# Feature transposes in the attention's banks, and an earlier scale for w_gu, in a one-core hybrid attention and mLSTM step

## The chip, the cores and the metric

The kernel runs on one core of a Trainium2 chip. The metric is the device time of one execution in microseconds (us), lower is better; the kernel before takes 1528.98 us as the median of three runs (1525.18 to 1530.79).

The core has five engines with an instruction queue each, executed in order: TensorE (PE in the profile, with its weight loads listed apart as PEld), VectorE (DVE), ScalarE (ACT), GpSimd (POOL) and SyncE (SP), which in this kernel mostly issues transfers. Results of matmuls land in PSUM, eight banks of 512 float32 values per partition, and are read from there by DVE or ACT. A bank that holds something unread can't take the next product.

## The reference

One layer of a diffusion backbone on 128 context tokens and 1024 latent tokens, width 1024, all in float32:

```
h   = rmsnorm(x) * (1 + sc1) + sh1
aq, ak, av, mq, mk, mv, mo, mg = split(h @ w_in)
o   = softmax(rope(aq) . rope(keys)) . vals          # 8 query heads, 2 key/value heads of 64
hm  = mlstm(mq, mk, mv, mg), both directions         # 4 heads of 128, chunks of 128 tokens
x   = x + g1 * (concat(o, rmsnorm(hm) * sigmoid(mo)) @ w_out)
h2  = rmsnorm(x) * (1 + sc2) + sh2
g, u = split(h2 @ w_gu)                              # 2 x 2816 columns
x   = x + g2 * ((silu(g) * u) @ w_down)
y   = rmsnorm(x)
```

Returned are y for both groups of tokens and, for the context, the keys and values and the mLSTM states. Float32 accuracy is kept by splitting an operand into a high part and a low rest and adding three products (high times high, high times low, low times high).

## The kernel before

The 1152 tokens are nine blocks of 128, in three chunks of three blocks. Chunk 0 holds the context block; in the code the chunks' rows are `cur` (chunk 0), `nxt` (chunk 1) and `far` (chunk 2).

**The order of the instructions.** The kernel is a Python program that emits instructions; a planner then fixes the order on every engine when the program is built. It simulates the engines with its own costs and takes, where several instructions are ready, the one that was emitted first. `with hot(n)` makes instructions count as if emitted n instructions earlier. PSUM banks and SBUF buffers are slots of pools; a tile waits for its slot until all readers of the tile before it are through. At run time the order is fixed and every engine waits at the head of its queue. Which pieces of work are emitted next to each other is written by hand: `weave(main, side, n_main, n_side)` goes through the steps of `main`, each of which reports its size in units, and after each draws as many steps from `side` as are due, n_side for n_main units.

**The feed-forward of chunk 0** (`groups`) goes in five groups of 4, 4, 4, 5 and 5 column blocks f. For each f, `gate_up` makes two products (L1473 to L1475, 24 matmuls of 384 tokens each, 6 units), each in a bank of its own, then tanh on ACT (L1491), two DVE steps (L1492, L1493) that read both banks, and the split of the result (L1496 and L145). After each group `down` (L1215 to L1217) multiplies with w_down in two halves of 512 columns; a half of five column blocks is 45 matmuls in three blocks of 15: block 0 first, then blocks 1 and 2 side by side in two banks. In steps it reports, the first three belong to block 0 and the last three to blocks 1 and 2. `add_gated` (L1204, L1205) reads the bank and adds to the rows.

**Weights** come in pieces: a transfer into one of two raw buffers, a rounding copy on ACT (L174), the rest on DVE (L145). Five pieces have a home at a time. For w_gu, ACT also sums absolute values of each piece (L178, `jk`, into `wsum`), with a line from the pool `t2`, which has three buffers and also holds the normalised half lines `y` of the features and the products of `add_gated`.

**The second feed-forward**, of chunks 1 and 2 together, works on both chunks with seven products of half-size operands in float16 (`pair6`, L1620 to L1622) instead of eight. It needs two things. `features6` turns each block's normalised rows over: for each half of 512 columns ACT scales a line y (L1554), four PE transposes (L124) put it into one PSUM bank, and ACT and DVE read four pieces of it into F (L1562, L1564); sums and differences of the chunks' F go to the operand tile Bt. `weights6` makes the weights' sums and, with a common scale, their float16 parts (L1606, L1607). That scale is made by `weight_scale`: a maximum over wsum (L1540), a PE transpose of it, a maximum over the result (L200), four tiny DVE steps (L190 to L193), a product that spreads the result over the partitions (L204), a copy (L205) and three more tiny steps (L1542 to L1544).

**PSUM.** During the attention and until the end of chunk 0's feed-forward the eight banks are: three for the scores S of one head (`psum["S"]`), one for the attention's product with the values (`psum["po"]`), and four that `bank()` hands out in turn to everything else. The attention of the last chunk of queries (`att`) is emitted in full before the part that the diff touches; its probabilities are turned by transfers (phT, plT), and its output is read from po by ACT (L1156) and DVE (L1158).

**The part that changes** is woven so: `main` is group 4 of chunk 0 (90 units), the gate/up of group 5 (60 units) and the first half of its down products (15 units), 165 in all. `side` is some empty steps (fillers), then `feats`: `features6` for the three blocks of nxt (12 steps), the output projection of far (`attn_out`, L1251 to L1255, 7 steps), and `features6` for the three blocks of far (18 steps). After it come the second half of the down products, the scale, the first weights of the second feed-forward and that feed-forward itself.

Of the kernel before, what the change touches and what calls it, by code (L numbers as in the profile page):

```python
# [8 lines left out]
F32 = mybir.dt.float32  # L9
# [10 lines left out]
P = 128  # L20
# [16 lines left out]
GROUPS = [(0, 4), (4, 4), (8, 4), (12, 5), (17, 5)]  # L37
# [5 lines left out]
NG = 3  # L43
# [6 lines left out]
def hybrid_step(ctx: ExitStack, tc: tile.TileContext, I: dict, O: dict):  # L50
# [11 lines left out]
    def nm(s):  # L62
        uid[0] += 1
        return f"{s}_{uid[0]}"

    def weave(main, side, n_main, n_side):

        due = 0.0
        for units in main:
            due += n_side / n_main * (units or 1)  # L70
            while due >= 1.0:
                next(side, None)
                due -= 1.0

    def emit(gen):
        for _ in gen:
            pass

    def chain(*gens):
        for g in gens:  # L80
            for v in g:
                yield v
# [22 lines left out]
    psum = {"mm": es_b.enter_context(tc.tile_pool(name="pB", bufs=4, space=PSUM, reuse_waits="tile"))}  # L105
# [3 lines left out]
    def bank():  # L109
        turn_of[0] += 1  # L110
        at = psum["mm"] if "mm1" not in psum or turn_of[0] % 4 else psum["mm1"]
        return at.tile([P, 512], F32, name=nm("mm"), tag="mm")
# [31 lines left out]
    def sub(out, full, hi, eng):  # L144
        (dve if eng == "dve" else pool).tensor_tensor(out=out, in0=full, in1=hi, op=ALU.subtract)  # L145
# [11 lines left out]
    def load_piece(srcs, shape, raw=None, own=None, tally=None):  # L157

        a, b = shape
        n = a * b  # L160

        def view(t):
            return t[:, :n].rearrange("p (a b) -> p a b", b=b)

        raw = raw_tile() if raw is None else raw
        if not own:
            loaded["n"] = (loaded["n"] + 1) % len(piece_tags)
            tag = piece_tags[loaded["n"]]
            at = homes.get(tag, wp)
            own = [at.tile([P, 1024], F32R, name=nm(t), tag=tag, bufs=2) for t in ("whi", "wlo")]  # L170
        hi, lo = own
        for part, ap_ in srcs:
            loaded["piece"] = dma(part(view(raw)), ap_).ins
        nc.scalar.copy(hi[:, :n], raw[:, :n])  # L174
        sub(lo[:, :n], raw[:, :n], hi[:, :n].bitcast(F32), "dve")
        if tally is not None:
            jk = ft.tile([P, D], BF16, name=nm("jk"), tag="t2", bufs=nt2[0])
            act(jk[:, :n], hi[:, :n].bitcast(F32), AF.Abs, accum_out=wsum[:, tally : tally + 1])  # L178
        return view(hi), view(lo)
# [160 lines left out]
    ps = bank()  # L340
# [3 lines left out]
    ps = bank()  # L344
# [1132 lines left out]
    def gate_up(a, f0, nf):  # L1477
        th, tl = a["h2"]
        acts = a["act"] = []
        for f in range(f0, f0 + nf):  # L1480
            if True:
                pg, pu = bank(), bank()
                for off, ps in ((0, pg), (D_FF, pu)):
                    src = w_gu[f + (NF if off else 0)].rearrange("p (k n) -> p k n", k=KD)
                    wh, wl = load_piece([(full_view, src)], (KD, P), tally=2 * f + (off > 0))
                    products(ps[:, 0:CT], wh, wl, th, tl)
                    yield 6
                parts = [(slice(0, CT), pg[:, 0:CT], pu[:, 0:CT])]
            tn = fp.tile([P, CT], F32, name=nm("tn"), tag="tn", bufs=2)
            for cs, g, u in parts:  # L1490
                act(tn[:, cs], g, AF.Tanh, scale=0.5)  # L1491
                dve.scalar_tensor_tensor(out=tn[:, cs], in0=tn[:, cs], scalar=1.0, in1=u, op0=ALU.add, op1=ALU.mult)  # L1492
                dve.tensor_tensor(out=tn[:, cs], in0=tn[:, cs], in1=g, op=ALU.mult)  # L1493
            hl = hlp.tile([P, 2, CT], F32R, name=nm("hl"), tag="hl", bufs=5)
            ah, al = hl[:, 0], hl[:, 1]
            nc.scalar.copy(ah, tn)  # L1496
            sub(al, tn, ah.bitcast(F32), "pool")
            acts.append((ah, al))

    def down(c, a, f0, nf, n):  # L1500
        g = gate_bc(1, c, n)
        acts = a["act"]
        pieces = []
        for j in range(0, nf, 2):
            m = min(2, nf - j)
            rows = w_down[(f0 + j) * P : (f0 + j + m) * P, n * 512 : (n + 1) * 512].rearrange("(a p) n -> p a n", p=P)
            pieces.append(load_piece([(full_view, rows)], (m, 512)))
        yield from three_blocks(
            lambda k, i: (acts[k][0][:, i * P : (i + 1) * P], acts[k][1][:, i * P : (i + 1) * P]),
            pieces, nf, lambda i, ps: add_gated(a["x1"][i], ps, g(c * CB + i), n))  # L1510
# [27 lines left out]
    def weight_scale():  # L1538

        dve.tensor_reduce(out=six[:, 7:8], in_=wsum, axis=AX.X, op=ALU.max)  # L1540
        emit(power_scale(fp, ones, six[:, 7:8], six[:, 2:4]))
        dve.tensor_tensor(out=six[:, 4:5], in0=six[:, 1:2], in1=six[:, 3:4], op=ALU.mult)  # L1542
        dve.tensor_tensor(out=six[:, 6:7], in0=six[:, 4:5], in1=six[:, 4:5], op=ALU.mult)
        dve.tensor_scalar(out=six[:, 5:6], in0=six[:, 4:5], scalar1=0.5, scalar2=None, op0=ALU.mult)  # L1544

    def features6(a, c, i, Bt, firsts):

        x1, r = a["x1"][i], a["rs"][i]
        at = slice(i * P, (i + 1) * P)
        F = a4p.tile([P, KD, P], F32, name=nm("F"), tag="A4", bufs=7)  # L1550
        for half in range(2):
            with hot(600):
                y = t2()
                act(y, x1[:, half * 512 : (half + 1) * 512], AF.Copy, scale=r)  # L1554
                ps = bank()
                for j in range(4):
                    transpose(ps[:, j * P : (j + 1) * P], y[:, j * P : (j + 1) * P])
                for j in range(4):
                    k = half * 4 + j
                    s, t = mods6[:, k, 0:1], mods6[:, k, 1:2]  # L1560
                    if j == 0:
                        act(F[:, k], ps[:, j * P : (j + 1) * P], AF.Identity, scale=s, bias=t)  # L1562
                    else:
                        dve.tensor_scalar(out=F[:, k], in0=ps[:, j * P : (j + 1) * P], scalar1=s, scalar2=t, op0=ALU.mult, op1=ALU.add)  # L1564
            yield
        for half, b in ((0, B11), (1, B21)) if c == 1 else ((1, B22),):
            v = F[:, half * 4 : half * 4 + 4]
            with hot(600):
                nc.scalar.copy(Bt[:, b, 0, :, at], v)
                sub(Bt[:, b, 1, :, at], v, Bt[:, b, 0, :, at], "dve")  # L1570
            yield
        if c == 1:
            firsts.append(F)
            return
        first = firsts.pop(0)
        T = sp.tile([P, 4, 4, P], F32, name=nm("T"), tag="S", bufs=1)
        with hot(600):
            dve.tensor_tensor(out=T[:, T1], in0=first[:, 0:4], in1=F[:, 0:4], op=ALU.subtract)
            dve.tensor_tensor(out=T[:, T2], in0=F[:, 4:8], in1=T[:, T1], op=ALU.add)
            dve.tensor_tensor(out=T[:, T3], in0=F[:, 0:4], in1=F[:, 4:8], op=ALU.subtract)  # L1580
            dve.tensor_tensor(out=T[:, T4], in0=first[:, 4:8], in1=T[:, T2], op=ALU.subtract)
        yield
        for j in (0, 2):
            with hot(600):
                nc.scalar.copy(Bt[:, j : j + 2, 0, :, at], T[:, j : j + 2])
                sub(Bt[:, j : j + 2, 1, :, at], T[:, j : j + 2], Bt[:, j : j + 2, 0, :, at], "dve")
            yield
# [162 lines left out]
    ps = bank()  # L1750
# [36 lines left out]
    cur, nxt = {}, {}  # L1787
# [11 lines left out]
    def groups(c, a, lst):  # L1799
        for f0, nf in lst:  # L1800
            yield from gate_up(a, f0, nf)
            yield from down(c, a, f0, nf, 0)
            yield from down(c, a, f0, nf, 1)
# [13 lines left out]
    main = groups(0, cur, GROUPS[:NG])  # L1817
    with tc.issue_after(loaded["gate"]):
        for _ in range(4):
# [10 lines left out]
    firsts = []  # L1830
    feats = chain(*[features6(nxt, 1, i, Bt, firsts) for i in range(CB)],
                  attn_out(far, o2, g_d[0, 1], lambda i: mixing(a4p, "A4", 7), o_d[CB:]), *[features6(far, 2, i, Bt, firsts) for i in range(CB)])
    main = chain(groups(0, cur, GROUPS[NG:-1]), gate_up(cur, *GROUPS[-1]), down(0, cur, *GROUPS[-1], 0))
    weave(main, chain([None] * 10, feats), 18 * sum(nf for _, nf in GROUPS[NG:-1]) + 15 * GROUPS[-1][1], 54)
    emit(feats)
    main = down(0, cur, *GROUPS[-1], 1)
    next(main)
    weight_scale()
    first_ops = weights6(0)
    emit(main)  # L1840
    es_f.close()
# [80 lines left out]
```

## Time and profile before

| what | value |
|---|---|
| median of three runs | 1528.98 us (1525.18 to 1530.79) |
| the profiled execution | 1527.74 us, span on the core 1526.0 us |
| PE busy | 1427.3 us, 94% of the span |
| DVE, ACT, POOL busy | 1129.1, 813.6, 218.4 us |
| granted PE clock, mean | 0.979 of full speed |

The span is the time from the first to the last instruction on the core; what the execution takes beyond it, 1.7 us, lies around it. The profile gives times from the span's start. A row of the timeline is the start, the length (of one or several instructions merged), engine, source line, operation, and in brackets how long the engine stood idle before and what it waited for. A row of the waits is who waited for whom, the total, the count and the longest.

### The profile page before, as it was taken

What the parts mean: (1) busy time and instruction counts of PE and PEld (TensorE: products, weight loads), DVE (VectorE), ACT (ScalarE), POOL (GpSimd) and SP (SyncE); (2) the same over time, 40 slices, a digit from 0 to 9 for tenths busy, and PEclk for the clock granted to TensorE, in tenths of its full rate; (3) what the DMA queues carried; (4) which work ended last, traced back from release to release, by engine and by line L of the source; (5) the groups of instructions that cost most, each with busy time, mean ns of one, the idle gap of its engine ahead of it and who ended that gap; (6) DMA issues with size and microseconds to landing.
All of it is one profiled execution on the core that took longest, in us unless ns stands there. A gap on an engine that the chain in (4) does not pass through costs nothing. (4 is left out here: it accounts for less than half of the span.)

```text
span 1526.0 us, 22787 instructions
## 1 busy us (share of the span) xinstructions
PE 1427.3 (94%) x8282; PEld 1064.8 (70%) x8282; DVE 1129.1 (74%) x2280; ACT 813.6 (53%) x1525; POOL 218.4 (14%) x310
## 2 busy tenths in 40 slices
PE   6889999998899889999999988989999999999994
PEld 3635667766677667978998977966766667676763
DVE  4978556775867878658678766969877696986857
ACT  5855467956767546555675944735233150523233
POOL 0122423232224335210100100100000000000000
PEclk9999999999999899999999999999999999999997
DMA  9575224553668764768687745334122130412112
GB/s 374 155 222 180 79 70 76 127 109 59 103 146 174 180 207 112 202 173 216 177 194 175 172 128 159 104 117 166 56 83 84 41 125 1 139 49 76 35 35 83
DMA packets 254182, 197.02 MB, mean 129 GB/s; under 512 B 166830, under 2 KB 208006, under 8 KB 254070
## 3 DMA queue, kind: packets, MB, share of 16 engines
q1 hardware_dynamic: 251070, 189.56, 45.8%
q10 hardware_dynamic: 2872, 5.62, 1.1%
q8 instruction: 65, 1.06, 0.3%
q14 instruction: 47, 0.39, 0.1%
q0 software_dynamic: 128, 0.39, 0.1%
HBM read 143.94 MB, written 13.26 MB: 103 GB/s over the span
## 5 line engine op out<-in xcount | busy, mean ns | idle before, releaser
L1621 PE MATMUL mm<-Bt,A 128*128 128x384 f16 x616 | 200.8, 326 | 0.0
L1620 PE MATMUL mm<-Bt,A 128*128 128x384 f16 x616 | 199.4, 326 | 0.5 <-DVE c L1641 0.5
L1622 PE MATMUL mm<-Bt,A 128*128 128x384 f16 x616 | 197.5, 326 | 0.0
L174 ACT CAST whi<-raw 128x1024 fp32r<-128x1024 f32 (+1 forms) x102 | 103.0, 1013 | 134.2 <-DMA raw<-in_w_down_dram 43.9
L145 DVE TENSOR_TENSOR wlo<-raw,whi 128x1024 fp32r<-128x1024 f32 (+1 forms) x102 | 121.3, 1190 | 52.9 <-ACT whi L174 50.5
L1136 DVE SCALAR_TENSOR_TENSOR pl<-pr,st,ph 128x1152 f16<-128x1152 f32 (+1 forms) x72 | 95.2, 1322 | 40.8 <-ACT ph L1135 40.8
L1473 PE MATMUL mm<-aTh,whi 128*128 128x384 f32 x352 | 121.3, 345 | 2.4 <-DVE tn L1492 1.2
L1474 PE MATMUL mm<-aTl,whi 128*128 128x384 f32 x352 | 120.2, 342 | 0.0
L1475 PE MATMUL mm<-aTh,wlo 128*128 128x384 f32 x352 | 120.0, 341 | 0.0
L1132 ACT ACTIVATE pr<-S,st 128x1152 f32<-128x1152 f32 (+1 forms) x72 | 81.5, 1132 | 51.8 <-DVE st L1131 50.5
L1131 DVE TENSOR_REDUCE st<-S 128x1 f32<-128x1152 f32 (+1 forms) x72 | 88.9, 1234 | 21.5 <-PE S L1129 21.4
L526 PE MATMUL wi<-headw,hT 128*128 128x384 f16 x288 | 93.9, 326 | 1.2 <-ACT th L816 1.2
L527 PE MATMUL wi<-headw,hT 128*128 128x384 f16 x288 | 93.9, 326 | 0.0
L528 PE MATMUL wi<-headw,hT 128*128 128x384 f16 x288 | 93.9, 326 | 0.0
L1135 ACT ACTIVATE ph<-pr,st 128x1152 f16<-128x1152 f32 (+1 forms) x72 | 83.7, 1163 | 17.1 <-DVE st L1134 8.5
L1129 PE MATMUL S<-kst,qT 128*128 128x384 f32 (+1 forms) x400 | 86.7, 350 | 3.6 <-ACT pr L1132 3.6
L1620 PEld LDWEIGHTS <-A 128*128 128x128 f16 x616 | 60.2, 98 | 42.5 <-issue 3.5
L1622 PEld LDWEIGHTS <-A 128*128 128x128 f16 x616 | 60.3, 98 | 39.8
L1621 PEld LDWEIGHTS <-A 128*128 128x128 f16 x616 | 60.3, 98 | 39.6 <-issue 0.6
L1606 ACT ACTIVATE A<-S,six 128x1024 f16<-128x1024 f32 x44 | 49.9, 1145 | 71.0 <-PE mm L1622 54.0
L1204 DVE TENSOR_TENSOR t<-mm,hmr 128x512 f32<-128x512 f32 x84 | 54.3, 683 | 41.0 <-PE mm L1690 33.3
L145 POOL TENSOR_TENSOR hl<-tn,hl 128x384 fp32r<-128x384 f32 x22 | 29.8, 1355 | 335.5 <-ACT hl L1496 307.9
(460 smaller groups left out, 3737.8 us busy)
## 6 DMA issues: line engine op xcount, KB each, us to landing
raw<-in_w_gu_dram SPq DMA_DIRECT2D x88, 512.0 KB, 3.4
raw<-in_w_down_dram SPq DMA_DIRECT2D x40, 512.0 KB, 3.8
a<-in_w_ada_dram SPq DMA_DIRECT2D x24, 512.0 KB, 5.6
iraw<-in_w_in_dram SPq DMA_DIRECT2D x32, 256.0 KB, 3.4
x<-in_x_sample_dram SPq DMA_DIRECT2D x11, 512.0 KB, 6.0
raw<-in_w_out_dram SPq DMA_DIRECT2D x10, 512.0 KB
aw<-in_w_ada_dram SPq DMA_DIRECT2D x8, 512.0 KB, 5.3
aw<-in_w_ada_dram SPq DMA_DIRECT2D x16, 256.0 KB, 7.8
```

The costliest lines, as they stand in the source:

```text
L145: (dve if eng == "dve" else pool).tensor_tensor(out=out, in0=full, in1=hi, op=ALU.subtract)
L174: nc.scalar.copy(hi[:, :n], raw[:, :n])
L526: mm(ps[:, :n], ah, wh[:, k % 2, c0 : c0 + n], start=(k == 0), stop=False)
L527: mm(ps[:, :n], ah, wl[:, k % 2, c0 : c0 + n], start=False, stop=False)
L528: mm(ps[:, :n], al, wh[:, k % 2, c0 : c0 + n], start=False, stop=(k == KD - 1))
L1136: dve.scalar_tensor_tensor(out=plv, in0=prv, scalar=st[:, 3:4], in1=phv, op0=ALU.mult, op1=ALU.subtract)
L1473: mm(ps, wh[:, k, :], th[:, k, :], start=(k == 0), stop=False)
L1474: mm(ps, wh[:, k, :], tl[:, k, :], start=False, stop=False)
L1475: mm(ps, wl[:, k, :], th[:, k, :], start=False, stop=(k == KD - 1))
L1620: mm(ps, wh[:, k], bt[:, 0, k], start=first and k == 0, stop=False, skip_group_check=True)
L1621: mm(ps, wh[:, k], bt[:, 1, k], start=False, stop=False, skip_group_check=True)
L1622: mm(ps, wl[:, k], bt[:, 0, k], start=False, stop=k == 3, skip_group_check=True)
```

## The change

Two functions change.

`features6` no longer takes its bank from `bank()`. For the first and third block of a chunk it takes the whole score tile S, three banks, and puts its two halves into the first two; for the second block it takes po, once for each half. Since S and po have one buffer each, a block waits for the readers of the one before it in the same place, and the first blocks wait for the attention's last readers. The tile S is asked for outside of `hot`.

In the main function the scale of w_gu is computed at another place: instead of behind the first step of the second half of the last down products, it is emitted behind the fourth step of the first half, that is when block 0 is through and blocks 1 and 2 have begun. The first weights (`weights6(0)`) stay where they were. And the pacing of `weave` changes: 6 fillers instead of 10, and 48 steps of `side` per 165 units instead of 54.

```diff
@@ features6
         F = a4p.tile([P, KD, P], F32, name=nm("F"), tag="A4", bufs=7)
+        wide = psum["S"].tile([P, 3, 512], F32, name=nm("S"), tag="S") if i % 2 == 0 else None
         for half in range(2):
             with hot(600):
                 y = t2()
                 act(y, x1[:, half * 512 : (half + 1) * 512], AF.Copy, scale=r)
-                ps = bank()
+                ps = wide[:, half] if i % 2 == 0 else psum["po"].tile([P, 512], F32, name=nm("po"), tag="po")
                 for j in range(4):
                     transpose(ps[:, j * P : (j + 1) * P], y[:, j * P : (j + 1) * P])
@@ hybrid_step
-    main = chain(groups(0, cur, GROUPS[NG:-1]), gate_up(cur, *GROUPS[-1]), down(0, cur, *GROUPS[-1], 0))
-    weave(main, chain([None] * 10, feats), 18 * sum(nf for _, nf in GROUPS[NG:-1]) + 15 * GROUPS[-1][1], 54)
+
+    def scaled_down():
+        for i, units in enumerate(down(0, cur, *GROUPS[-1], 0)):
+            if i == 3:
+                weight_scale()
+            yield units
+
+    main = chain(groups(0, cur, GROUPS[NG:-1]), gate_up(cur, *GROUPS[-1]), scaled_down())
+    weave(main, chain([None] * 6, feats), 18 * sum(nf for _, nf in GROUPS[NG:-1]) + 15 * GROUPS[-1][1], 48)
     emit(feats)
     main = down(0, cur, *GROUPS[-1], 1)
     next(main)
-    weight_scale()
     first_ops = weights6(0)
     emit(main)
```

## The prediction

> **What bounds the kernel now.** I read the page's busy table first, then busy time and granted clock stage by stage, then what TensorE (PE) waits for where it is idle.
>
> ```profile
> PE 1427.3 (94%) x8282; PEld 1064.8 (70%) x8282; DVE 1129.1 (74%) x2280; ACT 813.6 (53%) x1525; POOL 218.4 (14%) x310
> ```
>
> PE is the bound, so the edit is worth the PE idle time it removes or adds, with any low clock behind that. The windows view has start:end, length, busy time per engine, granted clock, DMA share and GB/s. Its first rows are the stages that the diff touches, its last four are short runs of one kind of matmul.
>
> ```profile
> 880.00:899.00 19.00, 12.67 (x70) 11.28 (x69) 12.35 (x28) 9.90 (x17) 1.02 (x1) 0.91 0.57 132
> 899.00:939.00 40.00, 40.00 (x181) 32.54 (x179) 26.64 (x40) 14.01 (x20) 1.33 (x1) 1.00 0.41 132
> 939.00:954.00 15.00, 8.99 (x45) 8.68 (x45) 11.14 (x25) 10.87 (x17) 0.00 (x0) 0.89 0.55 175
> 954.00:997.00 43.00, 42.72 (x245) 41.41 (x244) 35.92 (x54) 30.12 (x49) 7.59 (x4) 1.00 0.30 98
> 997.00:1022.00 25.00, 20.12 (x75) 15.19 (x74) 15.09 (x30) 6.63 (x11) 1.02 (x1) 0.86 0.26 78
> 894.86:898.30 3.44, 3.44 (x11) 3.44 (x12) 3.44 (x9) 2.38 (x5) 0.00 (x0) 0.51 0.00 0
> 939.90:944.29 4.39, 4.39 (x24) 4.08 (x24) 4.36 (x8) 3.93 (x6) 0.00 (x0) 1.00 0.60 202
> 998.87:1007.20 8.33, 8.33 (x36) 6.76 (x37) 2.60 (x5) 1.13 (x2) 1.02 (x1) 1.00 0.39 126
> 1015.32:1020.60 5.28, 5.28 (x13) 4.14 (x13) 3.03 (x6) 4.88 (x6) 0.00 (x0) 0.50 0.01 3
> ```
>
> PE is full in 899 to 939 and nearly in 954 to 997. Three holes stand out: A at 880 to 899 (19.00 - 12.67 = 6.3 us idle), B at 939 to 954 (6.0), C at 997 to 1022 (4.9). The waits view of PE names them (total us, times, longest), for 880 to 899 and then for 899 to 1022:
>
> ```profile
> PE mm L124 <- DVE F L1564: 2.5, 1, 2.5
> PE po L1153 <- DMA phT<-ph: 1.5, 1, 1.5
> PE po L1154 <- DMA plT<-pl: 1.0, 1, 1.0
> PE mm L1473 <- DVE tn L1492: 0.9, 1, 0.9
> PE mm L1473 <- DVE F L1564: 0.3, 1, 0.3
> ```
>
> ```profile
> PE mm L124 <- ACT t L1554: 5.1, 1, 5.1
> PE mm L204 <- DVE pv L193: 2.7, 1, 2.7
> PE mm L1215 <- DVE tn L1492: 1.3, 1, 1.3
> PE mm L1473 <- DVE t L1204: 0.9, 1, 0.9
> PE mm L1215 <- DVE t L1204: 0.9, 1, 0.9
> ```
>
> In A, 2.5 + 0.3 + 0.9 = 3.7 us are waits for a bank to be emptied, and 2.6 us the last attention product (po) waiting for its transposed probabilities. B is a feature transpose waiting for its normalised line y (L1554). In C, 2.7 us is L204, the product that spreads the w_gu scale, waiting for the last of four tiny DVE steps.
>
> **The change, part 1: the banks.** The next rows are one line's instructions each (count, min/median/max ns, first to last start): feature transposes between 860 and 890, the last exp that reads S, the feature evacuations, and the last readers of po. The fifth, from PE's timeline, is the end of the last scores (start, length).
>
> ```profile
> L124 PE MATMUL mm<-ident,t x12: 270/272/273, 862.8 to 886.3; 128*128 128x128 f32 x12
> ```
> ```profile
> L1132 ACT ACTIVATE pr<-S,st x1: 1226/1226/1226, 881.2 to 881.2; 128x1152 f32<-128x1152 f32 x1
> ```
> ```profile
> L1564 DVE TENSOR_SCALAR F<-mm,mods x9: 399/401/408, 892.7 to 895.3; 128x128 f32<-128x128 f32 x9
> ```
> ```profile
> L1158 DVE SCALAR_TENSOR_TENSOR oS<-po,vsc,ol x4: 332/344/344, 880.3 to 892.3; 64x128 f32<-64x128 f32 x4
> ```
> ```profile
> 877.70 0.86 PE L1129 MATMUL S<-kst,qT 128*128 128x384 f32 x4
> ```
>
> Twelve transposes, three halves, sit in three of the four rotating banks from 862.8 on, and DVE empties none before 892.7. Meanwhile gate/up, which takes two banks for each f, has what is left. With the edit these halves go to S and po and the four banks stay with the main work: the 3.7 us of bank waits go. In the 2.6 us of waiting for transposed probabilities another gate/up product could run (24 matmuls, 4.39 us at 939.90), if the planner places it ahead; the trace can't show that, so between 0 and 2.6 I take half, 1.3. A's low clock: 12 weight loads' worth took 3.44 us at 0.51 where 24 take 4.39, so 3.44 - 2.20 = 1.2 us lost; with 1.3 us idle left, like the 1.3 us wait in C whose next stretch, from 998.87, is at 1.00, I count it back whole. Two waits are new and stand in PE's queue ahead of all that follows: block 0 must wait for S until 881.2 + 1.2 = 882.4, blocks 1 for po until 892.6. Each costs between nothing (other products placed ahead) and, for S, 882.4 - 878.6 = 3.8 us from the last scores' end, for po 1.3 us (an estimate: the two reads of 0.34 and the copy before them); the nearest rows are the two waits of today's 12 halves, (2.5 + 5.1) / 12 = 0.6 each, so 1.2 for both. **A: 3.7 + 1.3 + 1.2 - 1.2 = 5.0 us gained**, bounds -1.4 (3.7 less both new waits at their worst, low clock kept) and 7.5 (3.7 + 2.6 + 1.2). No instruction is added; evacuations and their readers stay the same.
>
> **Part 2: the pacing.** Before, 10 fillers and 37 feature steps are due at 54 per 165 units (0.327), after, 6 at 48 (0.291). The first feature step moves from unit 11 / 0.327 = 33.6 to 7 / 0.291 = 24.1, the first step of far's from 91.7 to 89.4, the last from 143.6 to 147.8. A unit is 4.39 / 6 = 0.7 us, so these are 7 us earlier, 2 earlier, 3 later. Far's features in B thus keep their place, and their y waits for the same output projection. I take 0 for B; bounds 5.1 lost or gained.
>
> **Part 3: the scale.** Rows of the scale's tile and of DVE's timeline:
>
> ```profile
> L200 DVE TENSOR_REDUCE pv<-mm x1: 272/272/272, 1010.0 to 1010.0; 1x1 f32<-1x128 f32 x1
> L190 DVE TENSOR_SCALAR pv<-pv x1: 134/134/134, 1012.0 to 1012.0; 1x1 f32<-1x1 f32 x1
> L191 DVE TENSOR_SCALAR pv<-pv x1: 133/133/133, 1013.9 to 1013.9; 1x1 int32<-1x1 int32 x1
> L192 DVE TENSOR_SCALAR pv<-pv x1: 133/133/133, 1014.6 to 1014.6; 1x1 int32<-1x1 int32 x1
> L193 DVE TENSOR_SCALAR pv<-pv x1: 131/131/131, 1014.6 to 1014.6; 1x1 f32<-1x1 f32 x1
> ```
> ```profile
> 1003.73 0.69 DVE L145 TENSOR_TENSOR wlo<-raw,whi 128x512 fp32r<-128x512 f32 x1 [4.33 <-ACT whi L174]
> ```
>
> The five steps are 0.27 + 4 x 0.13 = 0.8 us of work and take from 1010.0 to 1014.7, because add-gated rows and the weight sums of the first pair stand between them in DVE's order. All ten DVE steps, two matmuls and one transpose move to the first half, behind the first block; no DMA moves, since the loads of the first pair (L1594) stay behind the second half's start. There DVE has 4.33 us of idle time in front of 1003.73, so the steps fit in, and PE has the rest of 90 down products before it needs anything of the scale. Gone: 2.7 us and the low clock behind it, 13 products in 5.28 us at 0.50 where 36 take 8.33: 5.28 - 3.01 = 2.3. In the new place L204 may wait between 0 and the 4.3 us for which DVE stood behind that weight row; nearer to 0, as PE passes some products between transpose and L204: 0.5. The bound and scale tiles take two rotating banks for a time while blocks 1 and 2 hold two; the 0.9 and 1.3 us waits for banks in C stay. **C: 2.7 + 2.3 - 0.5 = 4.5 us**, bounds -1.6 and 7.2.
>
> [...]
>
> **Sum.** 5.0 + 0 + 4.5 = 9.5 us. The profiled execution took 1527.74 us, so 1518.2; it lies 1.2 under the median of the runs, 1528.98, so the median goes to **1519.5**. Its own range: half of each step's distance to its bounds (3, 2.5 and 3), added as independent, is 5, so 1514.5 to 1524.5.
>
> **Rivals.**
> 1. *The hole at A only changes its name.* F is not emptied before 892.7 in either kernel, so S and po stay full as long as the banks did, and PE's queue, written in advance, meets S and po instead of F. For: L1132 and L1158 rows end late. Against: gate/up no longer needs those banks. A gains nothing: 1528.98 - 4.5 = 1524.5. Chance 0.14.
> 2. *L204 waits in its new place too*, at about the 2.7 us and 2.3 of today, because DVE's order again puts long rows between the tiny ones. Only A: 1524.0. Chance 0.12.
> 3. *B shrinks too*, because gate/up's next product, with free banks, is placed ahead of the far transposes: up to 5.1 more, 1514.4. Chance 0.12.
> 4. *The low clock does not follow the holes.* Without the 1.2 and 2.3 us the gain is 6.0: 1523.0. [...] The windows at 894.86 and 1015.32, each right behind a wait, speak against it. Chance 0.05.
> 5. *Slower: the y lines starve the weights.* Each y takes one of three half-line buffers, shared with the |w| sums (jk, L178), until its transpose has run.
>
> ```profile
> L178 ACT ACTIVATE jk<-whi x5: 1048/1057/1057, 846.4 to 872.3; 128x1024 bf16<-128x1024 f32 x5
> ```
> ```profile
> L1554 ACT ACTIVATE t<-x,ry x6: 710/720/732, 847.4 to 887.3; 128x512 f32<-128x512 f32 x6
> ```
> ```profile
> ACT jk L178 <- PE mm L124: 2.4, 2, 2.0
> ```
> ```profile
> L174 ACT CAST whi<-raw 128x1024 fp32r<-128x1024 f32 (+1 forms) x102 | 103.0, 1013 | 134.2 <-DMA raw<-in_w_down_dram 43.9
> L145 DVE TENSOR_TENSOR wlo<-raw,whi 128x1024 fp32r<-128x1024 f32 (+1 forms) x102 | 121.3, 1190 | 52.9 <-ACT whi L174 50.5
> ```
> ```profile
> raw<-in_w_gu_dram SPq DMA_DIRECT2D x88, 512.0 KB, 3.4
> ```
>
> The first y is made at 847.4, 15 us before the first transpose at 862.8, and jk already waits 2.4 us. Now y comes up to 7 us sooner and its transpose not before 882.4. A piece whose jk is held keeps its weight buffer; five are in flight. If three pieces of gate/up can't be loaded before 882.4, their 3 x 4.39 us of PE work and one supply (3.4 + 1.0 + 1.2) fall into A: 13.2 + 5.6 + 1.2 - 7.5 = 12.5 us more, less C's 4.5: 1537.0. It decides from two such pieces on (+8.1 against 4.5). Against: five sums are left at 846.4, all done by 873.4. Chance 0.10.
>
> **Chances.** My forecast has 0.47. About 0.5% (7.6 us: under 1521.3, over 1536.6) is what a measurement of this kernel tells from no change. Faster: 0.47 x 0.72 + 0.12 + 0.31 x 0.25 = 0.54. Slower: 0.8 of rival 5 and 0.01 for the rest, 0.09. Same: 0.37. The range reaches from rival 3 with its bounds, 1511, over 1 and 2 to 1530.
>
> **What would show it.** Right: feature transposes between 862 and 882 gone, no wait of L124 or L1473 for L1564 or L1492 at 880 to 899, granted clock there near 1.00; L204 behind the first block without a wait over 1 us and the last 15 down products at 0.23 us each. Wrong: a wait of L124 for L1132 or L1158 of more than 2 us; L204 waiting for L193 again; |w| sums behind 882 with weight casts waiting for them; a larger wait at the far transposes, which I took as unchanged.

## The result, and the profile after

The changed kernel takes 1515.14 us as the median of four runs (1512.59 to 1516.30), against 1527.91 us for the kernel before (1525.18 to 1530.79). The ratio is 0.9911, with a 95% interval from 0.9888 to 0.9933: 12.8 us faster. Its profiled execution took 1516.1 us with a span of 1514.3 us; before it was 1526.0 us, so the span is 11.7 us shorter. One run of all those reported below was disturbed, a run of "scale alone" that took 2087 us at a granted clock of 0.653: its ratio leaves it out, and without it the median there would be 1523.65 instead of 1523.82.

The windows view of the changed kernel for the same stretches (start:end, length, busy time of PE, PEld, DVE, ACT, POOL, granted clock, DMA share, GB/s):

```profile
880.00:899.00 19.00, 19.00 (x107) 17.00 (x107) 7.09 (x16) 7.57 (x12) 2.04 (x2) 1.00 0.29 62
899.00:939.00 40.00, 33.11 (x139) 25.62 (x138) 30.58 (x50) 18.15 (x30) 0.00 (x0) 0.91 0.43 145
939.00:954.00 15.00, 14.28 (x78) 13.51 (x77) 10.46 (x23) 8.95 (x14) 0.87 (x1) 1.00 0.56 175
954.00:997.00 43.00, 43.00 (x243) 40.99 (x242) 39.44 (x63) 35.52 (x58) 7.05 (x5) 1.00 0.37 123
997.00:1022.00 25.00, 23.65 (x125) 16.30 (x124) 23.31 (x46) 11.69 (x16) 0.00 (x0) 1.00 0.51 169
```

Holes A, B and C are nearly shut, but 899 to 939, which was full before, now has 6.9 us of idle PE at a clock of 0.91. To add this up I call a stage's **loss** its idle PE time plus its length times what the granted clock lacks to 1. Before: A 6.3 + 19 x 0.09 = 8.0, B 6.0 + 15 x 0.11 = 7.7, C 4.9 + 25 x 0.14 = 8.4, and 0.3 in 954 to 997; together 24.4 us. After: 6.9 + 40 x 0.09 = 10.5 in 899 to 939, 0.7 in B, 1.35 in C; together 12.6. The difference is 11.8 us, the span's 11.7: the whole gain lies in these 142 us. (The low clock also covers idle time, so this is a measure, not an exact sum. Profiled again, the changed kernel has 10.3 us in 899 to 939 and 12.4 in all. The kernel before has 7.0 and 7.1 in A, 0.9 twice in 899 to 939, 6.6 and 8.3 in B, 1.6 twice in 954 to 997, and 7.1 twice in C. A single stage is thus known to 1 or 2 us.)

What PE waits for there, in the waits view of 880 to 1022 (who waited for whom, total us, times, longest):

```profile
PE S L124 <- DVE F L1565: 4.4, 1, 4.4
PE mm L1215 <- DVE t L1204: 1.4, 1, 1.4
PE mm L1251 <- ACT mx L1418: 1.3, 1, 1.3
PE mm L1473 <- DVE tn L1492: 0.7, 1, 0.7
PE po L124 <- DVE F L1565: 0.6, 1, 0.6
PE mm L1251 <- ACT whi L174: 0.5, 1, 0.5
```

Gone are the bank waits in A, the two waits of po for its transfers, the 5.1 us of the far transposes for their line (B), and the 2.7 us of L204 for L193 (C). New is a transpose into S that waits 4.4 us, with waits of the output projection (L1251) behind it. The timeline of PE at that place, and the window behind it:

```profile
903.88 0.60 PE L124 MATMUL S<-ident,t 128*128 128x128 f32 x4
908.89 0.96 PE L124 MATMUL S<-ident,t 128*128 128x128 f32 x4 [4.41 <-DVE F L1565]
911.20 2.07 PE L1251 MATMUL mm<-whi,mx 128*128 128x512 f32 x4 [1.35 <-ACT mx L1418]
```
```profile
909.80:916.00 6.20, 4.85 (x13) 3.79 (x13) 5.76 (x11) 4.94 (x9) 0.00 (x0) 0.51 0.59 200
```

So one hole of some 6 us was left, with 6 us of half clock behind it. The |w| sums and the weight copies of the changed kernel, one line's instructions each (count, min/median/max ns, first to last start):

```profile
L178 ACT ACTIVATE jk<-whi x6: 1047/1052/1057, 845.1 to 904.4; 128x1024 bf16<-128x1024 f32 x6
```
```profile
L174 ACT CAST whi<-raw x2: 1040/1042/1044, 885.2 to 906.9; 128x1024 fp32r<-128x1024 f32 x2
```

The last sums of w_gu run until 904.4 + 1.05, where all were done by 873.4 before: the lines are held, as rival 5 said (that it is the lines is shown further down, by the run with lines of its own), and between 885.2 and 906.9 no piece of weights is copied; in the kernel before two started in that time, at 886.0 and 900.7. The price is in the hole and not in the supply of gate/up. The hole ends at L1251, whose operand mx ACT makes (L1418), and that operand comes at the same time in the kernel before and in the changed one:

```profile
L1418 ACT CAST mx<-t x3: 615/616/622, 910.7 to 912.9; 128x512 fp32r<-128x512 f32 x3
```
```profile
L1418 ACT CAST mx<-t x3: 612/617/618, 910.5 to 912.6; 128x512 fp32r<-128x512 f32 x3
```

(The first row is of the kernel before, the second of the changed one.) With A's waits gone PE is there first, and has to wait.

### The profile page after: what moved, and what is told of

Its sections match the earlier page's. It is cut to its first block, busy times and chain, and to the rows that moved or that the text cites. A ratio compares the mean times of both kernels' runs of the same rounds, so it can differ in the third digit from the quotient of the medians.

```text
span 1514.3 us, 22779 instructions
## 1 busy us (share of the span) xinstructions
PE 1422.5 (94%) x8282; PEld 1060.5 (70%) x8282; DVE 1130.3 (75%) x2280; ACT 812.0 (54%) x1525; POOL 215.4 (14%) x310
## 4 chain that ended last, share of the span: by engine, by line
PE 51%; DVE 9%; DMA 3%; ACT 3%; issue 2%; POOL 0%; SPq 0%; DVEq 0%; ACTq 0%; POOLq 0%
PE mm L1621 5%; PE mm L1622 5%; PE mm L1623 5%; PE mm L1689 4%; PE mm L1690 4%; PE mm L1691 4%; PE mm L1473 3%; PE mm L1475 3%; PE mm L1474 3%; PE S L1129 2%; PE mm L1215 2%; PE mm L1216 2%; PE mm L1217 2%; PE mm L1251 1%; PE mm L1253 1%
## 5 line engine op out<-in xcount | busy, mean ns | idle before, releaser
L1132 ACT ACTIVATE pr<-S,st 128x1152 f32<-128x1152 f32 (+1 forms) x72 | 81.4, 1131 | 53.3 <-DVE st L1131 52.0
L1689 PE MATMUL mm<-whi,hl 128*128 128x512 f32 x192 | 76.8, 400 | 0.0
```

Of the source, the lines that this page charges most:

```text
L1689: mm(ps, hl[:, 0, sl], wh[:, k % 2, :], start=(k == 0), stop=False)
```

## The experiments

Each kernel of the table was timed against runs of the kernel before on the same chip. The losses in us (as above, from each kernel's windows) stand beside the medians; "gain" is by the medians, for the changed kernel against 1527.91 and else against 1526.84 for the first four, 1526.70 for "turns" and 1527.13 for the others.

| kernel | A | 899-939 | B | 954-997 | C | median | gain | ratio, 95% |
|---|---|---|---|---|---|---|---|---|
| before | 8.0 | 0 | 7.7 | 0.3 | 8.4 | 1527.91 | | |
| changed | 0 | 10.5 | 0.7 | 0 | 1.4 | 1515.14 | 12.8 | 0.9911 [0.9888, 0.9933] |
| banks alone | 0 | 13.8 | 0 | 0 | 4.1 | 1520.47 | 6.4 | 0.9957 [0.9940, 0.9974] |
| scale alone | 8.2 | 1.6 | 8.5 | 1.6 | 3.4 | 1523.82 | 3.0 | 0.9980 [0.9967, 0.9992] |
| pacing alone | 6.6 | 0.6 | 8.7 | 0.7 | 5.0 | 1528.19 | -1.4 | 1.0008 [0.9996, 1.0019] |
| changed, lines of its own | 0 | 5.4 | 0 | 1.3 | 0.5 | 1511.21 | 15.6 | 0.9899 [0.9881, 0.9917] |
| banks and scale | 0 | 12.9 | 1.1 | 0.3 | 0.3 | 1518.02 | 9.1 | 0.9940 [0.9921, 0.9960] |
| banks and pacing | 0 | 10.6 | 0.7 | 0 | 5.6 | 1519.51 | 7.6 | 0.9946 [0.9927, 0.9966] |
| before, lines of its own | 5.6 | 0.9 | 6.7 | 1.6 | 7.1 | 1524.16 | 3.0 | 0.9981 [0.9971, 0.9992] |
| own lines, old pacing | 0 | 7.1 | 0 | 0.9 | 1.4 | 1513.10 | 14.0 | 0.9903 [0.9881, 0.9924] |
| changed, halves in turns | 0.6 | 11.5 | 0.7 | 1.9 | 1.5 | 1518.84 | 7.9 | 0.9950 [0.9932, 0.9967] |

(Pacing alone has another 4.1 us of loss in 840 to 880, "turns" another 1.9 in 1022 to 1062, "banks alone" 1.1 there.)

### The three parts alone

**Banks alone.** The kernel before with the bank lines of the diff:

```diff
+        wide = psum["S"].tile([P, 3, 512], F32, name=nm("S"), tag="S") if i % 2 == 0 else None
...
-                ps = bank()
+                ps = wide[:, half] if i % 2 == 0 else psum["po"].tile([P, 512], F32, name=nm("po"), tag="po")
```

> The kernel before with the new banks alone; pacing (10 fillers, 54) and the scale's place as before. Theory: the banks empty hole A (880 to 899, 8.0 us with its low clock), move a hole of about 10 us to 900 to 924, and, by leaving gate/up its banks, let two of its products run ahead of far's first transposes, which closes hole B (7.7 us before, about 0.7 after); hole C stays. Sum -8.0 + 10.5 - 7.0 = -4.5: 1523.4 us. Rival: B closes through the pacing; then B stays here at about 7 us and the time is 1530 us.

Measured: 6.4 us faster, 1520.47 us where 1523.4 was expected. A and B closed as expected; C, expected to stay, fell to 4.1, as no low clock came behind L204's wait. Three rows of its windows, and its two largest waits:

```profile
880.00:899.00 19.00, 19.00 (x112) 16.89 (x110) 7.76 (x14) 10.29 (x15) 2.01 (x2) 1.00 0.50 120
899.00:939.00 40.00, 31.44 (x134) 24.31 (x133) 28.37 (x49) 15.05 (x24) 0.00 (x0) 0.87 0.40 126
939.00:954.00 15.00, 15.00 (x83) 14.18 (x82) 12.01 (x26) 7.83 (x12) 0.00 (x0) 1.00 0.56 192
```
```profile
PE mm L1251 <- ACT mx L1418: 5.2, 1, 5.2
PE mm L204 <- DVE pv L193: 3.3, 1, 3.3
```

The banks alone shut A and B, with the old pacing. B goes because more gate/up stands ahead of the far transposes: it runs from 942.54 until the first of them at 956.32, some three products, where before it was one product (939.90 to 944.29) and then the wait. And the banks alone bring the new hole in 899 to 939, here as a wait of the output projection for its operand mx. ACT in turn waits 2.9 us in front of mx for the transfer t<-o_d (L1416), which brings the attention's output back into a line of t2.

**Scale alone.** The kernel before with `scaled_down` and without `weight_scale()` in its old place:

```diff
+            if i == 3:
+                weight_scale()
...
-    weight_scale()
```

> The kernel before with the scale's new place alone. Theory: hole C falls from 8.4 us with its low clock to about 1.4 us, L204 waits for nothing, the last 15 down products run at 0.23 us; A and B as before: 1527.9 - 7.0 = 1520.9 us. Rival: without the freer banks the chain of tiny DVE steps stretches in the new place as it did in the old one, and L204 waits 2 us or more there, with low clock behind: 1526 to 1528 us.

Measured: 3.0 us faster, 1523.82 us, between the 1520.9 of the theory and the 1526 of its rival. L204 stands in the timeline without a wait, and still there is a low clock a little ahead of it, behind waits of only 1.31 and 0.32 us:

```profile
1003.03 0.27 PE L124 MATMUL mm<-ident,six 128*1 128x128 f32 x1 [1.31 <-DVE tn L1492]
1003.62 0.51 PE L1215 MATMUL mm<-whi,hl 128*128 128x512 f32 x1 [0.32 <-DVE tn L1493]
1009.56 0.38 PE L204 MATMUL mm<-pv,ones 1*128 1x2 f32 x2
```
```profile
1003.60:1008.00 4.40, 4.38 (x12) 3.47 (x13) 1.34 (x6) 1.13 (x2) 1.00 (x1) 0.61 0.32 119
```

The wait goes as forecast; the low clock that takes its place does not follow the size of a wait. The profiled execution took 1527.67 us, 3.9 over the median, so the median run may have less of it.

**Pacing alone.** The kernel before with two numbers:

```diff
-    weave(main, chain([None] * 10, feats), ..., 54)
+    weave(main, chain([None] * 6, feats), ..., 48)
```

> The kernel before with the pacing of 6 fillers and 48 steps alone. Theory: the pacing does little by itself, all three holes stay within 2 us of their size: 1526 to 1530 us. Rival: the pacing is what puts far's transposes behind gate/up, B closes: 1521 us.

Measured: no change that is clear of the noise, as expected; of the three holes only C is more than 2 us smaller than before (5.0). Its waits still have the far transposes for their line, L204 for L193, and the bank wait of A:

```profile
PE mm L124 <- ACT t L1554: 5.2, 1, 5.2
PE mm L204 <- DVE pv L193: 2.7, 1, 2.7
PE mm L124 <- DVE F L1564: 2.5, 1, 2.5
```

The three alone add up to 6.4 + 3.0 - 1.4 = 8.0 us, the whole change gives 12.8.

### Two parts at a time

**Banks and scale** (the changed kernel with the old 10 and 54):

> The changed kernel with the old pacing (10 fillers, 54): banks and scale alone. Theory: the two parts add, -6.4 us for the banks as measured alone and -3.0 us for the scale as measured alone: 1517.5 us; the rest to the changed kernel's 1515.1 us is pacing, which only pays once the transposes have banks of their own. Rival: the pacing is worth nothing here either, as alone, and this kernel equals the changed one within 1 us: then the scale is worth more than 3 us once the banks are free.

**Banks and pacing** (the changed kernel with `weight_scale()` back behind the first step of the second half):

> The changed kernel with the scale at its old place: banks and pacing. Theory: L204 waits about 3 us as with the banks alone and the time is 1518 us, 3 us over the changed kernel. Rival: the scale's place decides more with free banks, since the half clock behind L204's wait comes and goes: 1520 us or more.

Measured: gains of 9.1 and 7.6 us. The first, 1518.02 us, agrees with its theory; the second, 1519.51, lies between its theory (1518) and its rival (1520 or more). The windows of the first, then of the second:

```profile
899.00:939.00 40.00, 32.35 (x138) 25.34 (x137) 26.70 (x48) 15.74 (x26) 0.00 (x0) 0.87 0.37 115
997.00:1022.00 25.00, 24.73 (x123) 17.70 (x123) 21.26 (x36) 10.83 (x16) 1.72 (x1) 1.00 0.50 159
```
```profile
899.00:939.00 40.00, 33.01 (x137) 25.45 (x136) 31.64 (x51) 19.36 (x32) 0.00 (x0) 0.91 0.47 148
997.00:1022.00 25.00, 21.19 (x103) 14.39 (x102) 19.00 (x37) 8.58 (x12) 0.00 (x0) 0.93 0.43 148
```

Taking the scale's move back costs 1519.51 - 1515.14 = 4.4 us, all of it in C (5.6 against 1.4). Taking the pacing back costs 2.9 us, most of it in the new hole (12.9 against 10.5). By the gains, each against its own runs of the kernel before, the two are 5.2 and 3.7. With the other part taken back as well they are less: the scale's move is worth 1520.47 - 1518.02 = 2.5 us with the old pacing, the pacing 1520.47 - 1519.51 = 1.0 us with the scale in its old place. The intervals of these two and of the whole change touch or overlap, so the single differences are known to 2 or 3 us at best; the traces say where they are.

### What ends the new hole

**Lines of their own.** The changed kernel, with y in the two half-line buffers of the gate rows, instead of the three lines of t2 shared with the |w| sums. (They are not quite its own: the output projection's gate rows come into them too, at 905.78 and 914.06 in this run.)

```diff
-                y = t2()
+                y = xe.tile([P, 512], F32, name=nm("y"), tag="hmr", bufs=2)
```

> The changed kernel, with the features' normalised lines y in the two buffers of the gate rows instead of in t2, which the weight sums (jk) also use. Theory: in the changed kernel the lines of block 0 and 1 are held until S and po are free, the sums of the next pieces of w_gu wait behind them until after 900, their pieces keep their homes, no weight is rounded between 886 and 907, and so TensorE has nothing to do at 904 to 911. With lines of their own the sums are done by 882, weight copies go on between 886 and 907, and the hole at 899 to 924 (6.9 us idle, 3.6 us of low clock) falls under 4 us together: about 1508 us. Rival: the hole is what its wait says, the third block's transposes waiting for S because DVE empties it late; then sums and copies come earlier but the wait of 4.4 us stays, and the time is within 2 us of the changed kernel, 1513 to 1517 us.

The same line in the kernel before:

> The kernel before with only the features' lines y moved to the two buffers of the gate rows; transposes in the rotating banks, scale and pacing as before. Theory: the hole at 880 to 899 comes from the three banks that the transposes hold until 892, not from the lines, so it stays at about 6 us, and the time is within 2 us of 1526.8. Rival: the lines held the weights back there too, and freeing them alone gives 4 us or more: under 1523 us.

The same line in the changed kernel with the old pacing:

> The changed kernel with lines of their own for y and the old pacing (10 fillers, 54). Theory: what the pacing did with shared lines was to set when the lines were asked for, so with lines of their own it does nothing, and the time is that of own lines with the new pacing, 1511 us, within 1.5 us. Rival: the pacing sets when the features of the third chunk run beside gate/up, and the time is 1514 us or more.

Measured: 1511.21 us for the first, the lowest median of all, between the 1508 of the theory and the 1513 of the rival: the wait for S fell to 0.7 us, as only the theory had it, but the stage's loss not under 4 us. The window and the waits there, the sums and the weight copies:

```profile
899.00:939.00 40.00, 36.24 (x157) 28.70 (x156) 29.00 (x49) 16.98 (x28) 0.00 (x0) 0.96 0.38 128
```
```profile
PE mm L1251 <- ACT mx L1418: 2.3, 1, 2.3
PE S L124 <- DVE F L1565: 0.7, 1, 0.7
```
```profile
L178 ACT ACTIVATE jk<-whi x5: 1042/1050/1057, 847.8 to 868.1; 128x1024 bf16<-128x1024 f32 x5
```
```profile
L174 ACT CAST whi<-raw x5: 618/1038/1052, 886.3 to 906.0; 128x1024 fp32r<-128x1024 f32 x4, 128x512 fp32r<-128x512 f32 x1
```

The sums are through at 869, five weight copies start from 886 to 906, where the changed kernel has one at 885.2 and the next at 906.9, mx starts at 907.4 instead of 910.5, and the stage's loss falls from 10.5 to 5.4 us. Two things come sooner at once: the sums leave ACT's queue in front of mx, and the transfers t<-o_d, which need a line of t2 as well, are issued from 896.12 on instead of 905.54. The runs do not part the two. The median falls by 3.9 (the gain grows by 2.8), so sharing the lines cost the change some 3 to 4 us; the two ranges of runs overlap by 1 us. With the old pacing the time is 1513.10, 1.9 us more: over the 1.5 of that theory, under the 1514 of its rival, and the same within the intervals. Whether the pacing was worth something only because it set when the shared lines are asked for is not shown, as 1.9 us here and 2.9 with shared lines can't be told apart.

In the kernel before, the lines are worth 3.0 us, again between theory and rival: the waits of po in A go, its bank waits stay (loss of A 5.6, against 7.0 to 8.0 in the three profiles of the kernel before), and the 5.1 us of B and the 2.7 us of L204 stay as they were.

**Halves in turns.** The changed kernel, but the first half of every block goes to S and the second to po, so that no half follows the half before it into the same tile. (S is now also asked for inside of `hot`.)

```diff
-                ps = wide[:, half] if i % 2 == 0 else psum["po"].tile([P, 512], F32, name=nm("po"), tag="po")
+                ps = psum["S"].tile([P, 3, 512], F32, name=nm("S"), tag="S")[:, 0] if half == 0 else psum["po"].tile([P, 512], F32, name=nm("po"), tag="po")
```

> The changed kernel, but the halves take turns: the first half of every block in S (one of its banks), the second half of every block in po. In the changed kernel the last half of block 2 (908.89) runs right after the three DVE reads of the half before it in the same tile S (907.70 + 1.04 = 908.74), though that half lies in another bank, and its line y is ready at 906.1. Theory one (a tile of three banks is one thing to wait for: the second half waits for the readers of the first): with turns the last half waits only for po, read until 906.6, so the 4.4 us wait falls to about 2.2, the last transposes stand near 906.7, and the kernel is 2 us faster than the changed one, 1513. Theory two (the chain of lines y, sums and evacuations on ACT and DVE sets the time, and the tile only bears its name): the wait stays near 4.4 us under another name, and the time stays at 1515.

Measured: 1518.84 us, not faster than the changed kernel. PE's timeline there:

```profile
900.51 0.60 PE L124 MATMUL S<-ident,t 128*128 128x128 f32 x4
903.34 1.08 PE L124 MATMUL po<-ident,t 128*128 128x128 f32 x4 [2.23 <-ACT Bt L1569]
907.92 2.08 PE L1251 MATMUL mm<-whi,mx 128*128 128x512 f32 x4 [3.49 <-ACT mx L1418]
```

The wait of the last half fell from 4.41 to 2.23 us, as theory one had it, but the wait for mx behind it grew from 1.35 to 3.49: together 5.72 us, where it was 5.76. From the transposes before the hole to L1251 it takes 907.92 - 900.51 = 7.4 us, and 911.20 - 903.88 = 7.3 in the changed kernel. Theory two thus holds for the hole: it ends when ACT gets to mx (L1418), and the transposes only divide it. In front of mx stand on ACT three held sums, at 1.05 us each, and then two weight copies, the second of which waits 1.1 us for its transfer in the changed kernel. For the time neither theory holds: the kernel came out 3.7 us above the changed one. Its span is only 0.9 us longer, but its last exp of the attention (L1132) starts 3.4 us sooner (876.85 against 880.23), ahead of the first transposes. So 4.3 us are lost behind it. The losses put them in A (0.6), the hole (1.0), 954 to 997 (1.9) and 1022 to 1062 (1.9); why they are lost there stays open.

### The low clock, again

The kernel before twice more and the changed kernel once more, unchanged, each profiled and timed once:

> The kernel before, unchanged, profiled once more, to see whether the same holes bring the same low clock. In its first profile the stretches at about half clock stood at 894.9 to 898.3, in 939 to 954 and at 1015.3 to 1020.6 (windows 880 to 899 at 0.91, 939 to 954 at 0.89, 997 to 1022 at 0.86). If the size of a hole decides, the three windows show the same clocks again within 0.02, behind the same waits. If the low clock comes by a window that runs apart from the program, at least one of the three windows changes by 0.05 or more while the waits stay the same within 0.3 us, and the time changes by the low clock alone, some 1 to 2 us for each.

> As the run beside it: the kernel before, a third profile. If the size of a hole decides, the clocks of the three windows are again 0.91, 0.89 and 0.86; if a free window decides, they spread, with waits of the same lengths.

> The changed kernel, unchanged, profiled once more. Its first profile has one low stretch at 909.8 to 916.0 (0.51) behind the 4.4 us wait of a transpose for S, and 1.00 in 997 to 1022. If the size of a hole decides, 899 to 939 shows 0.91 again and 997 to 1022 shows 1.00. If a free window decides, the first may differ by 0.05, though behind the 4.4 us it is the likeliest of all to stay; 997 to 1022 stays at 1.00 in both, since there is no hole.

Measured: 1525.81, 1525.28 and 1514.81 us. The windows of the first of them, then of the second:

```profile
880.00:899.00 19.00, 13.76 (x75) 12.68 (x76) 11.00 (x24) 8.95 (x17) 1.02 (x1) 0.91 0.43 111
939.00:954.00 15.00, 10.02 (x52) 9.69 (x51) 11.34 (x27) 11.77 (x21) 0.00 (x0) 0.89 0.54 183
997.00:1022.00 25.00, 21.43 (x84) 16.11 (x85) 15.19 (x30) 7.16 (x10) 1.02 (x1) 0.86 0.34 108
```
```profile
880.00:899.00 19.00, 13.64 (x75) 12.42 (x74) 10.69 (x24) 8.83 (x16) 1.02 (x1) 0.91 0.39 102
939.00:954.00 15.00, 10.13 (x53) 9.78 (x52) 10.66 (x27) 12.02 (x21) 0.00 (x0) 0.77 0.55 173
997.00:1022.00 25.00, 21.41 (x85) 16.00 (x85) 15.22 (x31) 7.44 (x11) 1.02 (x1) 0.86 0.34 115
```

Eight of the nine clocks in three profiles of the kernel before are the same (0.91, 0.89, 0.86); the ninth is 0.77 instead of 0.89, though the wait in that window is no longer than in the others (4.9 us), and the execution is not longer either. The changed kernel has its 0.91 and 1.00 again:

```profile
899.00:939.00 40.00, 33.33 (x140) 25.74 (x139) 31.00 (x51) 18.82 (x30) 0.00 (x0) 0.91 0.43 145
997.00:1022.00 25.00, 23.64 (x128) 16.34 (x128) 23.28 (x44) 12.73 (x17) 0.00 (x0) 1.00 0.51 163
```

Within one kernel the low clock mostly repeats. Between kernels it does not go by the gap: "banks alone" and "banks and pacing" have the same wait of 3.32 us at L204, and the same 17 matmuls behind it:

```profile
1008.85 0.38 PE L204 MATMUL mm<-pv,ones 1*128 1x2 f32 x2 [3.32 <-DVE pv L193]
```
```profile
1008.85:1012.60 3.75, 3.75 (x17) 3.03 (x17) 2.50 (x6) 3.14 (x3) 0.00 (x0) 1.00 0.02 4
```
```profile
1007.25 0.38 PE L204 MATMUL mm<-pv,ones 1*128 1x2 f32 x2 [3.32 <-DVE pv L193]
```
```profile
1007.25:1012.60 5.35, 5.35 (x17) 4.16 (x17) 4.10 (x7) 4.74 (x6) 0.00 (x0) 0.68 0.24 80
```

The first has none, the second pays 5.35 - 3.75 = 1.6 us. Narrower windows show where the low clock lies: in "banks and pacing" at 0.50 for 3.41 us, and between 880 and 1022 in the first profile of the kernel before for 3.4, 3.4 and 6.8 us, in that of the changed kernel for 6.8 us:

```profile
1008.93:1012.34 3.41, 3.41 (x10) 2.63 (x9) 3.29 (x3) 3.41 (x5) 0.00 (x0) 0.50 0.27 86
```
```profile
894.95:898.37 3.42, 3.42 (x11) 3.42 (x12) 3.42 (x9) 2.36 (x5) 0.00 (x0) 0.50 0.00 0
949.57:952.98 3.41, 3.41 (x14) 3.41 (x14) 1.42 (x2) 3.41 (x6) 0.00 (x0) 0.50 0.44 154
1014.42:1021.25 6.83, 6.45 (x16) 5.19 (x17) 3.35 (x9) 4.88 (x6) 0.00 (x0) 0.50 0.01 2
```
```profile
909.03:915.86 6.83, 5.48 (x15) 4.12 (x15) 6.39 (x11) 5.02 (x8) 0.00 (x0) 0.50 0.66 227
```

With the wait of B (5.1, 5.0 and 4.9 us) came a low stretch in all three profiles of the kernel before, of 3.4 us in the first two. In the third it was 6.8 us, from 943.8 to 950.6, of which 2.9 us lay in the wait itself, which ended at 946.66, and cost nothing. So it is not the gap alone that decides; what does beside it is not shown. The expectation by the size of a hole thus fails in one window of nine, by 0.12 behind the same wait; that by a free window has this change of clock, but not the 1 to 2 us in the time that were to come with it. Why the window with the 2.7 us of L204 had 0.86 in all three executions stays open.

## Why the prediction came out as it did

The time, 1515.1, lies in the range, at the lower end of the forecast's own 1514.5 to 1524.5, and 4.4 us under the forecast. The sum is near, 9.5 forecast and 12.8 measured, but its terms are not: A with its new hole came out 7.5 us worse than forecast, B 7.0 better, C 2.5 better. That the first two nearly cancelled is luck. The signs of being right all came (no feature transpose between 862 and 882, a clock of 1.00 in 880 to 899, L204 at 997.82 without a wait), and one sign of being wrong came with them: |w| sums behind 882.

- **A, forecast 5.0.** Right: the waits of the transposes and of gate/up for each other's banks are gone from 880 to 899, and the clock there is 1.00. The stage gained all of its 8.0 us, with po's 2.6 us of waits, of which I had counted half. Wrong: the term of 1.2 us for new waits. They measured 4.4 us at S and 0.6 at po, with 1.9 us behind them at L1251 and the low clock, 10.5 us in all, in a stage that I had not looked at. Net, A and its new hole lost 2.5 us. I had looked at when S and po come free of the attention's last readers; that cost nothing, since gate/up went ahead. The waits came later, from a block's halves on each other and from ACT's work in front of mx, which was not ready sooner than before. This is rival 1 in part: the hole did change its name, and its place.
- **B, forecast 0.** Wrong by 7.0 us. I argued from the pacing, which indeed changes nothing alone. The cause is the one of rival 3: banks free, gate/up's next products stand ahead of the far transposes. "Banks alone" shows it with the old pacing. I had the mechanism with a chance of 0.12 only, and its time, 1514.4, is the nearest of all to the measured one. I had not seen that the shortage of banks in A could also be what put the far transposes so early in B.
- **C, forecast 4.5.** Right in mechanism: L204 has no wait in its new place, where I took 0.5 (with lines of its own it has 1.3). With free banks the step is worth 4.2 us in C's loss and 4.4 in the medians with the new pacing, 3.8 and 2.5 with the old one. Alone it gave 3.0; in its trace a low clock came behind other, smaller waits. In the whole change C gained 7.0, because free banks also cut C's waits for banks (2.2 us before, 0.7 with banks alone, 1.4 in the changed kernel) and its low clock (loss of C 8.4 before, 4.1 with banks alone, 5.6 with banks and pacing).
- **The low clock, 3.5 us of the 9.5.** That it goes with the holes was right as a sum over the kernel (24.4 to 12.6 with it, 17.5 to 9.0 without). For a single hole it can't be counted on, as the two waits of 3.32 us show. The window 997 to 1022 shows 0.86 in all three profiles of the kernel before, with a wait of 2.7 us at L204 in each.
- **Rival 5, slower.** Its mechanism happened: the sums were held to 905. Its price did not: some 3 to 4 us by the lines of their own, where I had put 13.2 + 5.6 + 1.2. Gate/up was not starved, as PE is full from 880 to 899; what stood behind the sums, and did not come sooner than before, is mx.

## What to carry to other kernels

Results that lie in a bank for 30 us before they are read (here from 862.8 to 892, with 3.7 us of waits for a bank) keep it from whatever else could run; when such a shortage goes, look for every hole that it makes, not only for the one where its name stands. A hole's end is set by what comes last of several things: before pricing the removal of one wait, follow the next consumer (here the output projection's operand on ACT) and see when it would be ready; if it comes no sooner than before, the gain ends there. Small shared buffers tie unrelated work together, and two buffers of its own for y were worth as much as one of the parts of this change.

## What the runs showed of the hardware that I had not expected

The low clock did not go by the length of a wait. Waits of 1.3 and 0.3 us were followed by 3.4 us at 0.50 in "scale alone" (an estimate from 0.61 over 4.40 us), and one of 3.3 us by nothing in "banks alone" and by 3.41 us at 0.50 in "banks and pacing". Such a stretch of 3.41 us costs 1.7 us (an estimate: half of it; the 17 matmuls behind L204 took 1.6 longer in "banks and pacing" than in "banks alone") where PE is busy through it, and nothing where it waits: the same gap of 4.9 to 5.1 us gave a window's mean of 0.89 twice and 0.77 once, without a longer time. A hole's price from one trace is thus uncertain by 2 us or so.
